# A mixing stage re-ordered in front of a stream of expert weights: modulation sums on TensorE, gate norm on VectorE, attention beside u's projection

## The chip, the cores and the metric

The kernel runs on one core of a Trainium2 chip. The engines of the core are TensorE (PE, matrix products; its weight loads are listed as PEld), VectorE (DVE), ScalarE (ACT), GpSimd (POOL) and SyncE (SP), which in this kernel only issues DMAs, in the order in which they stand in its program. The metric is the time of one execution in microseconds; lower is better. The kernel before takes 1545.3 us (median of three runs, 1542.98 to 1547.39).

## The reference

The reference is one encoder block for 512 tokens of 1024 channels, in float32. Cut to what matters:

```python
mod = silu(c) @ w_ada + b_ada                 # 6 x 1024: shift1, scale1, gate1, shift2, scale2, gate2
h   = rms_norm(x) * (1 + scale1) + shift1
q, k, v, u, g = split(h @ w_in)               # 512, 128, 128, 512, 512 columns
attn = windowed_attention(q, k, v, sink)      # 8 heads, 2 of keys, blocks of 128 tokens and their neighbours
gm   = gelu(u) * (W_s @ layer_norm(gelu(g)) + b_s)      # per chunk of 128 tokens, 8 channel groups
mix  = concat(rms_norm(attn), rms_norm(gm))
x    = x + gate1 * rms_norm(mix @ w_out)
h2   = rms_norm(x) * (1 + scale2) + shift2
aff  = softmax(h2 @ w_router)                 # 16 experts, each takes its 64 best tokens
y    = sum over experts of aff * (silu(xs @ w_gate) * (xs @ w_up)) @ w_down
out  = x + gate2 * rms_norm(y)
```

Each of the 16 experts has three matrices of 1024 x 2816 floats, so the weights of the experts make nearly all of the 593.6 MB that are read from HBM.

## The kernel before

The program has two stages. The first (to about 261 us) holds everything up to the router. The second runs the 16 experts one after the other; for each, the weights come in chunks of 1408 KB (128 partitions x 2816 floats), TensorE multiplies the chosen rows by them, and the chunk's buffer is then free for a later chunk.

**Buffers of the weights.** There are 13 slots in four pools: `sl` (6 slots), `s2p` (3), `s3p` (3) and `s4p` (1). The first stage uses the same bytes: `sl` holds the rows of w_in, w_ada and w_out as they come in; the bytes of `s2p` are taken from the pool of the early phase (`ea`), and its three slots hold `wz`, the rows of w_out for the gMLP's half of the channels, split in two parts, until the last product with them (`project_z`); `s3p` takes over the bytes of the attention's pool `at`, and `s4p` those of `ow`, the output projection's pool. SP issues the chunks in the order of the program and waits at each until the slot's last reader is through (L835). Chunks 0 to 5 go into `sl`, 6 to 8 into `s2p`, 9 to 11 into `s3p`, 12 into `s4p`; 13 and 14 go into three places left over from the first stage (`in_places`, L931 and L932), and from chunk 15 on a slot has to be freed by an expert's product.

**The first stage.** Products that need float32's accuracy are made as three products of split operands (`mm3`, L346 to L348: high by high, low by high, high by low), each with 512 columns. In order of the program:

- `SEQ` orders, for each of the 8 groups k of 128 input channels, `m` (shift1 and scale1 of the group), `d` (the normed and modulated rows hh, hl) and `q` (the products for q, k, v, tile `qkp`). For k in `MODPE` the sums of `m` are products on TensorE (`mod1_rows`, L293, tile `pm`); for k = 4, 6, 7 they are a chain of eight sums on VectorE (`mod1_acc`, L315 and L317, tile `acc1`), which TensorE then only adds over the partitions (`mod1_cols`, L322).
- Eight units of g (tile `pg`, 12 products each), and beside them on VectorE the sums of the other four modulations (`mod2`, L553 and L555, tile `racc`: 8 instructions of 128x1024 for one of the four vectors); `mod2_cols` (L278, L285, L561 to L574) turns the finished sums into columns.
- Eight units of u (tile `pu`), the first four ahead of the attention and the last four in its steps 0 to 3. `gate_norm` is the layer norm of g, for each of four token blocks: BN_STATS and BN_AGGR, an inverse root of one column, a TENSOR_SCALAR (L505) on VectorE, and a product and a sum on GpSimd (L506, L507).
- A loop of 26 steps i. Steps 0 to 15 are `attn_scores`: block n = i // 4, heads j and j + 4 (products `sp` L430; mask and minimum on VectorE, L432; exponential on ScalarE, L435; the division by the sum on GpSimd, L439). Two steps later `attn_out` transposes the probabilities (`ptr`, L454) and multiplies them by v (`po`, L462). A table `todo` hangs the rest of the stage on steps: the rows of w_out (`OWS`), gelu, the spatial products and the change of pools (step 4), `gmlp_cols` and `project_z` (`ZC`), the end of a block's attention and its projection, the residual, the router's logits (`XC`) and, at `RS`, ranks of the first three blocks (`rank_part`, L806).
- `rsqrt` is an inverse root by a guess from the bits and three Newton steps on VectorE, 8 instructions for one column (L184, L186, L191, L196), 11 for more.

So each engine's order is the order in which the program is written; the numbers in the tables decide it, and an engine that waits holds up whatever stands behind.

Of the kernel before, what the change touches and what calls it, by code (L numbers as in the profile page):

```python
# [47 lines left out]
TINY = 2.0 ** -126  # L48


@with_exitstack
def encoder_block(ctx, tc, x, c, w_ada, b_ada, norm_pre_mix, norm_post_mix, w_in, sink, sgu_ln_g,
# [32 lines left out]
    # ---------------------------------------------------------------- loads  # L85
# [17 lines left out]
    # columns of w_ada for shift1, scale1 of 128 channels with the rows of w_in for q, k, v of these channels  # L103
# [18 lines left out]
    def more_loads():  # L122
# [15 lines left out]
        nc.sync.dma_start(lnb, sgu_ln_b.to_broadcast([P, DG]))  # L138
        wst = slot([NG, P], name="wst")
# [4 lines left out]
    # ---------------------------------------------------------------- constants  # L144
# [4 lines left out]
    ones = cp.tile([P, 1], F32, name="ones")  # L149
# [19 lines left out]
    def make_dist():  # L169
        """|distance|, or a huge number outside the window; keys in front of, of, behind the block"""  # L170
# [66 lines left out]
    # ---------------------------------------------------------------- x: transposed; 1 / rms  # L237
# [29 lines left out]
    # ---------------------------------------------------------------- shift1, scale1; h  # L267
# [7 lines left out]
    def mod_rows(pm, col, w, n, first, last):  # L275
        """w [P, 4, n]: four column tiles of the array add col^T w at once"""
# [4 lines left out]
    def mod_cols(rows, n):  # L281
        """the four rows of rows [P, n] as columns: [P, n / 128, 4] in PSUM"""
# [5 lines left out]
    def mod1_rows(k):  # L288
        """PE: even and odd rows of w_ada in column tiles of their own"""
# [17 lines left out]
    acc1 = {}  # L307

    def mod1_acc(k):
        """DVE: the sums over a partition's rows"""  # L310
        acc1[k] = t = ea.tile([P, 2, P], F32, name="acc1", bufs=2)
        for kk in range(KD):
            w = wq[k][0][:, :, kk]
            if kk == 0:
                nc.vector.tensor_scalar(t, w, cs[:, kk:kk + 1], None, op0=OP.mult)  # L315
            else:
                nc.vector.scalar_tensor_tensor(t, w, cs[:, kk:kk + 1], t, op0=OP.mult, op1=OP.add)  # L317

    def mod1_cols(k):
        pm = bank("pm")  # L320
        for j in range(2):
            nc.tensor.matmul(pm[32 * j:32 * j + 32, :P], ones.to_broadcast([P, 32]), acc1[k][:, j], start=True,  # L322
                             stop=True, tile_position=(0, 32 * j))
# [41 lines left out]
    for b in range(NB):  # L365
        sumsq(ssx[:, b:b + 1], x_sb[:, b], junk)
        if b == NB - 1:
            x_rsqrt(b, NB)
# [250 lines left out]
    for k in range(4):  # L619
        unit("u", k)  # L620
        if k < 2:
            mod2_cols(k)
# [462 lines left out]
```

## Time and profile before

| | |
|---|---|
| median of three runs | 1545.3 us (1542.98 to 1547.39) |
| span of the profiled execution | 1544.5 us |
| mean granted TensorE clock | 0.985 |
| TensorE busy | 1387.1 us, 90% |
| VectorE busy | 429.7 us, 28% |
| ScalarE, GpSimd busy | 188.9 us, 116.0 us |
| moved by DMA | 596.86 MB, mean 386 GB/s |

The span runs from the first to the last instruction of the profiled execution, and no time of its own beyond the span is given for it; the median of the timed runs lies 0.8 us above the span. Busy shares are means over two stages that have little in common: in the experts' stage the DMA engines move about 429 GB/s without a break, in the first stage they move between 7 and 355 GB/s. The rows further below are therefore mostly from stretches of the first stage.

### The profile page before, as it was taken

What the parts mean: (1) busy time and instruction counts of PE and PEld (TensorE: products, weight loads), DVE (VectorE), ACT (ScalarE), POOL (GpSimd) and SP (SyncE); (2) the same over time, 40 slices, a digit from 0 to 9 for tenths busy, and PEclk for the clock granted to TensorE, in tenths of its full rate; (3) what the DMA queues carried; (4) which work ended last, traced back from release to release, by engine and by line L of the source; (5) the groups of instructions that cost most, each with busy time, mean ns of one, the idle gap of its engine ahead of it and who ended that gap; (6) DMA issues with size and microseconds to landing.
All of it is one profiled execution on the core that took longest, in us unless ns stands there. A gap on an engine that the chain in (4) does not pass through costs nothing.

```text
span 1544.5 us, 17570 instructions
## 1 busy us (share of the span) xinstructions
PE 1387.1 (90%) x7282; PEld 619.8 (40%) x7282; DVE 429.7 (28%) x1087; ACT 188.9 (12%) x404; POOL 116.0 (8%) x144
## 2 busy tenths in 40 slices
PE   7888998999999998998898998989898989898986
PEld 5665665343444433333333333324242423333323
DVE  5789857112112120212112111112020303020104
ACT  3336433000010000000100000000000000000001
POOL 2457310000000000000000000000000000000002
PEclk9998999999999999999999999999999999999998
DMA  9776608999999999999999999999999999999995
GB/s 316 275 252 181 241 6 334 415 411 428 429 429 429 429 429 428 429 428 429 429 428 429 429 429 429 429 428 429 429 428 429 429 429 429 428 429 429 429 396 202
DMA packets 92711, 596.86 MB, mean 386 GB/s; under 512 B 8692, under 2 KB 31960, under 8 KB 44760
## 3 DMA queue, kind: packets, MB, share of 16 engines
q1 hardware_dynamic: 92632, 595.74, 93.3%
q8 instruction: 57, 0.93, 0.2%
q14 instruction: 22, 0.18, 0.0%
HBM read 593.62 MB, written 2.10 MB: 386 GB/s over the span
## 4 chain that ended last, share of the span: by engine, by line
DMA 60%; PE 28%; DVE 8%; issue 1%; ACT 1%; POOL 1%; SPq 0%; DVEq 0%; ACTq 0%; POOLq 0%
DMA w<-in_w_down_dram 23%; DMA w<-in_w_up_dram 19%; DMA w<-in_w_gate_dram 18%; PE pf L949 11%; PE pd L991 4%; PE px L888 1%; PE pys L1001 1%; PE py L348 1%; PE py L346 1%; PE po L462 1%; PE py L347 1%; DVE ex L851 1%; PE pd L1031 1%; DVE racc L555 1%; DVE acc L317 1%
## 5 line engine op out<-in xcount | busy, mean ns | idle before, releaser
L949 PE MATMUL pf<-w,ex 128*64 128x512 f32 (+1 forms) x3072 | 638.0, 561 | 42.0 <-DMA w<-in_w_up_dram 40.6
L949 PEld LDWEIGHTS pf<-w,ex 128*64 128x64 f32 x3072 | 215.0, 137 | 433.2 <-issue 326.2
L991 PE MATMUL pd<-w,ex 128*64 128x512 f32 (+1 forms) x1440 | 319.3, 563 | 33.7 <-DMA w<-in_w_down_dram 33.7
L991 PEld LDWEIGHTS pd<-w,ex 128*64 128x64 f32 x1440 | 109.9, 136 | 231.7 <-issue 126.0
L967 DVE TENSOR_TENSOR ex<-pf,ex 128x512 f32<-128x512 f32 (+1 forms) x48 | 30.4, 647 | 362.3 <-PE pf L949 362.0
L995 DVE TENSOR_SCALAR ex<-pd,gc 128x512 f32<-128x512 f32 x15 | 11.3, 751 | 377.6 <-PE pd L991 377.6
L907 POOL COPY ex<-ex 128x512 f32<-128x512 f32 x16 | 9.8, 613 | 1138.2 <-DVE ex L905 1058.0
L888 PE MATMUL px<-x_sb,ex 128*64 128x256 f32 x512 | 71.0, 386 | 8.6 <-DVE ex L864 7.4
L919 ACT ACTIVATE ex<-pot 128x512 f32<-128x512 f32 x16 | 9.6, 597 | 544.6 <-PE pot L917 544.6
L1007 DVE TENSOR_TENSOR y<-pys,y 128x512 f32<-128x512 f32 x112 | 68.2, 681 | 17.0 <-PE pys L1001 17.0
L974 ACT ACTIVATE ex<-pht 128x512 f32<-128x512 f32 (+1 forms) x48 | 23.5, 559 | 374.6 <-PE pht L973 374.6
L1001 PE MATMUL pys<-ex 64*128 64x512 f32 x240 | 55.6, 602 | 12.7 <-DVE ex L995 12.7
L900 DVE TENSOR_SCALAR ex<-pxt,mods 128x64 f32<-128x64 f32 x128 | 34.9, 337 | 92.0 <-PE pxt L895 92.0
L888 PEld LDWEIGHTS px<-x_sb,ex 128*64 128x64 f32 x512 | 41.3, 136 | 38.3 <-DVE ex L864 18.8
L851 DVE SCALAR_TENSOR_TENSOR ex<-rt,afs,before 128x512 f32<-128x512 f32 (+2 forms) x65 | 46.8, 719 | 12.3 <-PE rt L858 12.3
L913 DVE COPY gc<-pgc 128x1 f32<-128x1 f32 x16 | 2.5, 158 | 152.6 <-PE pgc L910 152.6
L555 DVE SCALAR_TENSOR_TENSOR racc<-ada,cs,racc 128x1024 f32<-128x1024 f32 x28 | 42.6, 1521 | 0.2
L959 ACT ACTIVATE ex<-pf 128x512 f32<-128x512 f32 (+1 forms) x48 | 26.9, 561 | 121.2 <-PE pf L949 120.4
L1001 PEld LDWEIGHTS pys<-ex 64*128 64x128 f32 x240 | 21.9, 186 | 47.1 <-DVE ex L995 25.9
L973 PE MATMUL pht<-ident,ex 128*128 128x128 f32 x176 | 25.7, 295 | 12.1 <-DVE ex L967 12.1
L973 PEld LDWEIGHTS pht<-ident,ex 128*128 128x128 f32 x176 | 22.7, 213 | 22.7 <-DVE ex L967 22.7
L890 ACT ACTIVATE ex<-px 128x256 f32<-128x256 f32 x32 | 12.3, 383 | 125.7 <-PE px L888 125.6
(254 smaller groups left out, 1086.3 us busy)
## 6 DMA issues: line engine op xcount, KB each, us to landing
w<-in_w_gate_dram SPq DMA_DIRECT2D x128, 1408.0 KB, 26.8
w<-in_w_up_dram SPq DMA_DIRECT2D x126, 1408.0 KB, 26.8
w<-in_w_down_dram SPq DMA_DIRECT2D x120, 1408.0 KB, 26.8
ada<-in_w_ada_dram SPq DMA_DIRECT2D x16, 1024.0 KB, 6.5
w<-in_w_down_dram SPq DMA_DIRECT2D x18, 512.0 KB, 9.6
wq<-in_w_ada_dram SPq DMA_DIRECT2D x16, 512.0 KB, 5.9
wi<-in_w_in_dram SPq DMA_DIRECT2D x4, 1024.0 KB, 5.2
wq<-in_w_in_dram SPq DMA_DIRECT2D x8, 384.0 KB, 6.2
```

Source lines behind the costliest of these rows:

```text
L555: nc.vector.scalar_tensor_tensor(acc[i], t[:, r], cs[:, k:k + 1], acc[i], op0=OP.mult, op1=OP.add)
L851: nc.vector.scalar_tensor_tensor(junk[:, :c1 - c0], p[:, c0:c1], afs[:, b, e:e + 1], before[:, o + c0:o + c1], op0=OP.subtract, op1=OP.is_ ...
L888: nc.tensor.matmul(px[i][h * CAP:(h + 1) * CAP, :256], ohr[:, b], x_sb[:, b, c0:c0 + 256], start=(b == 0), stop=(b == NB - 1))
L900: nc.vector.tensor_scalar(xs[:, k], pt[:, c0:c0 + CAP], s2[:, k:k + 1], sh2[:, k:k + 1], op0=OP.mult, op1=OP.add)
L949: nc.tensor.matmul(pb[n][h * 64:(h + 1) * 64, :NW[n]], XS[e][:, k], t, start=(i == 0), stop=(i == KD - 1))
L959: nc.scalar.activation(hid[:, n * 512:n * 512 + NW[n]], pg[n][:, :NW[n]], AF.Silu)
L967: nc.vector.tensor_tensor(hs, pu[n][:, :NW[n]], hs, op=OP.mult)
L973: nc.tensor.transpose(p[:, j * P:(j + 1) * P], hv[:, j0 + j], ident)
L974: nc.scalar.activation(hT[:, j0:j0 + n], p.rearrange("p (j t) -> p j t", j=4)[:, :n], AF.Copy)
L991: nc.tensor.matmul(pd[dh * 64:(dh + 1) * 64, c0:c0 + n], hT[:, j, h * CAP:(h + 1) * CAP], t[:, o - q * FF:o - q * FF + n], start=(h == 0 a ...
L1001: nc.tensor.matmul(p, OT[e][dh * 64:(dh + 1) * 64, b * P:(b + 1) * P], oe[dh * 64:(dh + 1) * 64, :], start=True, stop=True)
L1007: nc.vector.tensor_tensor(yb, p, yb, op=OP.add)
```

## The change

The changed kernel computes the same. The first stage is put together otherwise:

- `m` is made on TensorE for all eight groups; `mod1_acc`, `mod1_cols` and `MODPE` are gone.
- `mod2(0)` (gate1) is taken up into the q, k, v sequence (`a0` to `a3` in `SEQ`), `mod2(1)` and `mod2(2)` stand beside the units of g, and `mod2(3)` at steps 10 to 13 of the loop (before: 8, 8, 9, 9). The columns of gate1 are made in unit 2 of g, those of shift2 after unit 0 of u, those of scale2 at step 1.
- `gate_norm` takes the four blocks at once, all of it on VectorE, with one inverse root of four columns, after unit 0 of u.
- Two units of u, not four, stand ahead of the attention; the other six stand in steps 0 to 5, and gelu, the spatial products and the change of pools in step 6 (before: 4). `ZC`, `XC`, `OWS`, `GS` and the tables `AE` and `YC` give the other work new steps.
- `attn_out` keeps the transposed probabilities of two steps together, and multiplies them by v in products of 256 columns instead of 128, half as many.
- `rsqrt` takes -v/2 and makes one step of higher order and one Newton step: 6 instructions for one column, 8 for more. The inverse roots of x are taken for four blocks at once.
- The loads of `wst` and of g's first half are issued earlier; the tile `ones` is 160 bytes wide instead of 4, which moves the tiles behind it by 128 bytes. The four pools of weight slots keep their places.

The core of the diff (comments that went, and the same scaling of the argument of `rsqrt` at each of its calls, are left out):

```diff
-MODPE = (0, 1, 2, 3, 5)
-SEQ = "d0 m1 q0 d1 m2 d2 m3 q1 d3 m4 q2 d4 m5 q3 d5 m6 q4 d6 m7 q5 d7 q6 q7"
-M2 = (0, 0, 1, 1, 3)
-M3 = (8, 8, 9, 9, 10)
-GN = (None, None, 0, 0)
-GS, RS = 23, 21
+SEQ = "d0 m1 q0 d1 m2 d2 m3 q1 d3 m4 q2 d4 m5 q3 d5 m6 q4 d6 m7 a0 q5 d7 a1 q6 a2 q7 a3"
+U0 = 2
+GS, RS = 20, 21
+M3 = (10, 11, 12, 13, 15)
+GV = 7
+AE = (5, 11, 13)
+YC = (10, 12, 14, 17)
-ZC = (5, 6, 10, 12)
-XC = (10, 13, 18, 21)
-OWS = (5, 6, 4, 4)
+ZC = (7, 9, 11, 13)
+XC = (13, 15, 18, 21)
+OWS = (8, 9, 6, 7)
...
-    ones = cp.tile([P, 1], F32, name="ones")
+    ones = cp.tile([P, 40], F32, name="ones")[:, 0:1]
...
-            (mod1_rows if k in MODPE else mod1_acc)(k)
+            mod1_rows(k)
...
+            if j % 2 == 0:
+                pTs[g] = at.tile([P, 3, 2, P], F32, name="pT", tag="pT", bufs=2)
...
+        if j % 2:
+            for i in range(nk):
+                for g in range(2):
+                    nc.tensor.matmul(po[n, j][g * HD:(g + 1) * HD, (j - 1) * P:(j + 1) * P],
+                                     v_sb[:, k0 + i, g * HD:(g + 1) * HD], pTs[g][:, i].rearrange("p j q -> p (j q)"),
+                                     start=(i == 0), stop=(i == nk - 1))
...
-        nc.vector.tensor_scalar(v, v, mv[:, 0:1], r, op0=OP.subtract, op1=OP.mult)
-        nc.gpsimd.tensor_tensor(v, v, lng, op=OP.mult)
-        nc.gpsimd.tensor_tensor(v, v, lnb, op=OP.add)
+    def gate_norm():
+        mv = rs.tile([P, NB, 2], F32, name="mv", bufs=1)
+        for b in range(NB):
+            st = rs.tile([P, 6], F32, name="st")
+            nc.vector.bn_stats(st, vn[:, b])
+            nc.vector.bn_aggr(mv[:, b], st)
+            nc.vector.scalar_tensor_tensor(vn[:, b], vn[:, b], mv[:, b, 0:1], lng, op0=OP.subtract, op1=OP.mult)
+        h = rs.tile([P, NB], F32, name="hv", bufs=1)
+        nc.vector.tensor_scalar(h, mv[:, :, 1], EPS, -0.5, op0=OP.add, op1=OP.mult)
+        r = rs.tile([P, NB], F32, name="rln", bufs=1)
+        rsqrt(r, h, NB)
+        for b in range(NB):
+            v = vn[:, b]
+            nc.vector.scalar_tensor_tensor(v, v, r[:, b:b + 1], lnb, op0=OP.mult, op1=OP.add)
...
-        mod2(k // 4, k % 4)
+        mod2(1 + k // 4, k % 4)
+        if k == 2:
+            mod2_cols(0)
...
-    for k in range(4):
+    for k in range(U0):
         unit("u", k)
-        if k < 2:
-            mod2_cols(k)
-        if GN[k] is None:
-            gate_norm(k)
+        if k == 0:
+            mod2_cols(1)
+            gate_norm()
...
-    for k in range(4):
-        at_step(k, (unit, "u", k + 4))
-    at_step(4, (gelu, "u", us[0]), (spatial,), (swap,))
+    for k in range(U0, KD):
+        at_step(k - U0, (unit, "u", k))
+    at_step(1, (mod2_cols, 2))
+    at_step(KD - U0, (gelu, "u", us[0]), (spatial,), (swap,))
```

What stands where is seen in the order of the instructions. On VectorE, where steps 0 and 1 of the attention begin (`st` and `mv`, `vn` and `rln` belong to the gate norm, `racc` to the modulation sums, `pr,am` is the mask of one head pair's scores), the program of before reads:

```order
L432 ISA pr,am<-sp,dist,nsink 128x256
L432 ISA am 128x1
L191 SCALAR_TENSOR_TENSOR rs_t<-rs_y,rs_h 128x1
L555 SCALAR_TENSOR_TENSOR racc<-ada_1190,cs,racc 128x1024
L196 SCALAR_TENSOR_TENSOR rs_y<-rs_t,rs_y 128x1
L437 RECIPROCAL dn<-dn 128x2
L555 SCALAR_TENSOR_TENSOR racc<-ada_1190,cs,racc 128x1024
L191 SCALAR_TENSOR_TENSOR rs_t<-rs_y,rs_h 128x1
L196 SCALAR_TENSOR_TENSOR rs_y<-rs_t,rs_i 128x1
L555 SCALAR_TENSOR_TENSOR racc<-ada_1194,cs,racc 128x1024
L196 SCALAR_TENSOR_TENSOR rln<-rs_t,rs_y 128x1
L191 SCALAR_TENSOR_TENSOR rs_t<-rs_y,rs_h 128x1
```


and the changed program, at the same masks:

```order
L358 TENSOR_SCALAR racc<-ada_899,cs 128x1024
L537 BN_AGGR mv<-st 128x2
L463 ISA pr,am<-sp,dist,nsink 128x256
L463 ISA am 128x1
L360 SCALAR_TENSOR_TENSOR racc<-ada_899,cs,racc 128x1024
L538 SCALAR_TENSOR_TENSOR vn<-vn,mv,sgu 128x512
L360 SCALAR_TENSOR_TENSOR racc<-ada_920,cs,racc 128x1024
L540 TENSOR_SCALAR hv<-mv 128x4
L463 ISA pr,am<-sp,dist,nsink 128x256
L463 ISA am 128x1
L360 SCALAR_TENSOR_TENSOR racc<-ada_920,cs,racc 128x1024
L192 TENSOR_SCALAR rs_i<-hv 128x4
```


In the first, the norm's short instructions for one column stand among the sums of scale2, and the masks of step 0 come behind the statistics of all four blocks; in the second, the masks of step 0 come among the full-width products of the norm, whose one root of four columns follows.

On TensorE, at the last product with `wz`, which frees the last slot of `s2p` (`py` is the output projection, `sp` scores, `ptr` and `po` the attention's output, `pl` logits, `wo` the attention's rows of w_out), the program of before reads:

```order
L347 MATMUL py<-wz,mix 128x512
L348 MATMUL py<-wz,mix 128x512
L346 MATMUL py<-wz,mix 128x512
L347 MATMUL py<-wz_1409,mix 128x512
L348 MATMUL py<-wz,mix 128x512
L430 MATMUL sp<-qk 128x256 x2
L454 MATMUL ptr<-ident,pr 128x128 x4
L736 MATMUL pl_2283<-fold,rows 128x16
L346 MATMUL py<-wo,mix 128x512
L347 MATMUL py<-wo,mix 128x512
L348 MATMUL py<-wo,mix 128x512
```


and the changed one:

```order
L323 MATMUL py<-wz,mix 128x512
L324 MATMUL py<-wz,mix 128x512
L322 MATMUL py<-wz,mix 128x512
L323 MATMUL py<-wz_1462,mix 128x512
L324 MATMUL py<-wz,mix 128x512
L488 MATMUL ptr<-ident,pr 128x128 x4
L714 MATMUL pl<-hT,wsp 32x128 x8
L488 MATMUL ptr<-ident,pr 128x128 x4
L497 MATMUL po<-pT,v_sb 64x256
L722 MATMUL pl_2225<-fold,rows 128x16
L322 MATMUL py<-wo,mix 128x512
L323 MATMUL py<-wo,mix 128x512
```


Before, the scores of the last step (`sp`) stand behind the last product with `wz`; after, they stand ahead of it, and what is left behind it is a shorter rest: 24 products `py` up to the first expert, where it was 36.

## Rows read from the trace of the kernel before

**Rows 1.** Page, part 4: share of the chain that ended last, by engine

```profile
DMA 60%; PE 28%; DVE 8%; issue 1%; ACT 1%; POOL 1%; SPq 0%; DVEq 0%; ACTq 0%; POOLq 0%
```

**Rows 2.** Windows: stretch, length, busy us (x instructions) per engine, PEclk, DMA share, GB/s

```profile
194.00:230.00 36.00, 34.07 (x207) 24.39 (x206) 19.01 (x71) 14.19 (x38) 4.95 (x11) 0.91 0.00 1
230.00:252.00 22.00, 18.34 (x121) 13.32 (x119) 16.38 (x71) 9.75 (x29) 0.93 (x2) 1.00 0.97 383
252.00:254.00 2.00, 1.17 (x6) 1.20 (x7) 1.50 (x3) 1.20 (x3) 0.00 (x0) 0.71 0.27 113
...
400.00:1200.00 800.00, 730.70 (x3704) 284.53 (x3700) 142.83 (x341) 45.16 (x90) 6.13 (x10) 1.00 1.01 429
```

**Rows 3.** Waits of SP's queue, 150 to 275 us: total, times, longest

```profile
SPq L835 <- PE py L348: 49.2, 2, 48.8
SPq L835 <- DVE ty L806: 15.9, 1, 15.9
```

**Rows 4.** Timeline of SP, 225 to 270 us: start, us, line, transfer

```profile
229.85 1.93 SPq L835 DMA_DIRECT2D w<-in_w_gate_dram  x2
231.96 25.53 SPq L835 DMA_DIRECT2D w<-in_w_up_dram  x5
257.54 0.94 SPq L931 DMA_DIRECT2D w<-in_w_up_dram  x1
```

**Rows 5.** Windows of the first stage, columns as in rows 2

```profile
0.00:70.00 70.00, 55.88 (x370) 42.07 (x370) 43.19 (x108) 25.74 (x45) 23.50 (x44) 0.93 0.87 283
70.00:93.50 23.50, 23.32 (x102) 18.54 (x102) 15.91 (x12) 7.19 (x12) 15.15 (x10) 1.00 0.97 355
93.50:131.00 37.50, 32.72 (x152) 22.53 (x150) 37.30 (x77) 13.56 (x26) 22.79 (x16) 0.91 0.63 193
131.00:160.00 29.00, 23.42 (x182) 15.07 (x182) 26.66 (x67) 20.09 (x44) 18.33 (x22) 0.88 0.63 212
160.00:194.60 34.60, 34.09 (x203) 23.45 (x202) 28.80 (x87) 14.31 (x36) 9.91 (x14) 1.00 0.57 210
194.60:231.90 37.30, 35.37 (x211) 25.28 (x210) 19.45 (x73) 14.91 (x40) 4.95 (x11) 0.91 0.04 7
231.90:261.60 29.70, 22.41 (x159) 16.81 (x158) 22.76 (x101) 12.55 (x36) 0.93 (x2) 0.94 0.81 325
```

**Rows 6.** Waits of TensorE, 0 to 70 us: total, times, longest

```profile
PE pm L322 <- DVE acc L317: 4.5, 2, 2.6
```

**Rows 7.** Groups by line, 0 to 262 us: busy, mean ns, idle before

```profile
L555 DVE SCALAR_TENSOR_TENSOR racc<-ada,cs,racc 128x1024 f32<-128x1024 f32 x28 | 42.6, 1521 | 0.2
...
L317 DVE SCALAR_TENSOR_TENSOR acc<-wq,cs,acc 128x256 f32<-128x256 f32 x21 | 13.9, 663 | 0.5
...
L191 DVE SCALAR_TENSOR_TENSOR rs_t<-rs_y,rs_h 128x1 f32<-128x1 f32 x34 | 9.6, 282 | 0.5
...
L506 POOL TENSOR_TENSOR vn<-vn,sgu 128x512 f32<-128x512 f32 x4 | 7.1, 1778 | 4.9 <-DVE vn L505 3.8 <-DVE rs_y L196 0.7 <-DMA ada<-in_w_ada_dram 0.4
...
L293 PE MATMUL pm<-wq,cs 128*32 128x128 f32 x160 | 6.7, 289 | 0.8 <-DMA wq<-in_w_ada_dram 0.8
...
L505 DVE TENSOR_SCALAR vn<-vn,mv,rln 128x512 f32<-128x512 f32 x4 | 3.1, 778 | 0.0
```

**Rows 8.** Timeline of VectorE, 105 to 117 us: start, us, line, operation

```profile
105.74 1.27 DVE L555 SCALAR_TENSOR_TENSOR racc<-ada,cs,racc 128x1024 f32<-128x1024 f32 x1
...
109.56 1.21 DVE L191 SCALAR_TENSOR_TENSOR rs_t<-rs_y,rs_h 128x1 f32<-128x1 f32 x1
...
116.60 0.53 DVE L505 TENSOR_SCALAR vn<-vn,mv,rln 128x512 f32<-128x512 f32 x1
```

**Rows 9.** Timeline of TensorE at 200.6 us, columns as in rows 8

```profile
200.60 0.40 PE L346 MATMUL py<-wz,mix 128*128 128x512 f32 x1
200.84 0.40 PE L347 MATMUL py<-wz,mix 128*128 128x512 f32 x1
```

**Rows 10.** Window of 222 to 229.5 us, columns as in rows 2

```profile
222.00:229.50 7.50, 7.50 (x27) 6.23 (x24) 2.36 (x14) 0.40 (x2) 0.00 (x0) 0.54 0.00 0
```

More of the change, by code (lines that the diff above doesn't have):

```diff
@@ L305, in mod1_end @@
         nc.vector.tensor_tensor(sh1[:, k:k + 1], shift, pcol("ba", k), op=OP.add)
[L307 to L323, printed above, removed]
-        rows = rs.tile([P, P], F32, name="rows", bufs=1)[:64]
-        nc.vector.tensor_copy(rows, pm[:64, :P])
-        pt = bank("pt")
-        nc.tensor.transpose(pt[:, :64], rows, ident[:64, :64])
-        mod1_end(k, pt[:, 0:1], pt[:, 32:33])
     def modulate(k):
@@ L363, in qkv, with mod2 @@
             mm3(qkp[m], h[:, c0:c0 + P], l[:, c0:c0 + P], hh[k], hl[k], k == 0, k == KD - 1)
+    G0 = cp.tile([P, D], F32, name="G0")
+    mods = cp.tile([P, 4, 8], F32, name="mods")
+    g1c, sh2, s2, g2c = (mods[:, i] for i in range(4))
+    rb = cp.tile([P, NE], F32, name="rb")
+    acc = {}
+    def mod2(i, kk):
+        t = slot([2, D], name="ada2")
+        nc.sync.dma_start(t, ada[:, 2 * kk:2 * kk + 2, 2 + i])
+        if kk == 0:
+            acc[i] = (ea if i < 2 else at).tile([P, D], F32, name="racc")
+        for r in range(2):
+            k = 2 * kk + r
+            if k == 0:
+                nc.vector.tensor_scalar(acc[i], t[:, r], cs[:, k:k + 1], None, op0=OP.mult)
+            else:
+                nc.vector.scalar_tensor_tensor(acc[i], t[:, r], cs[:, k:k + 1], acc[i], op0=OP.mult, op1=OP.add)
@@ new lines, in mod2_cols @@
+    def mod2_cols(i):
+        pm = bank("pm2")
+        mod_rows(pm, ones, acc[i].rearrange("p (j w) -> p j w", j=4), 256, True, True)
+        rows = at.tile([P, 256], F32, name="rows2", tag="pT", bufs=2)
+        nc.vector.tensor_copy(rows, pm[:, :256])
+        m = mod_cols(rows, 256)
+        nc.vector.tensor_tensor(mods[:, i].rearrange("p (j q) -> p q j", j=4), m,
+                                pcol("ba", 16 + 8 * i, 8).rearrange("p (j q) -> p q j", j=4), op=OP.add)
+        if i == 0:
+            nc.vector.tensor_tensor(g1c, g1c, pcol("pom", 0, 8), op=OP.mult)
+            spread(G0, g1c)
+        elif i == 2:
+            nc.vector.tensor_tensor(s2, s2, pcol("npf", 0, 8), op=OP.mult)
+            pb = bank("pb")
+            for k in range(KD):
+                mod_rows(pb, sh2[:, k:k + 1], wr[:, k:k + 1].to_broadcast([P, 4, NE]), NE, k == 0, k == KD - 1)
+            nc.vector.tensor_scalar(rb, pb[:, :NE], -1.0, None, op0=OP.mult)
+            nc.vector.scalar_tensor_tensor(wsp[:, :, :NE], wr, -1.0, s2.unsqueeze(2).to_broadcast([P, KD, NE]),
+                                           op0=OP.mult, op1=OP.mult)
+        elif i == 3:
+            nc.vector.tensor_tensor(g2c, g2c, pcol("pof", 0, 8), op=OP.mult)
@@ L365, in encoder_block, with spread @@
+    def spread(dst, cols):
+        for i in range(2):
+            p = bank("spr")
+            for k in range(4):
+                kk = i * 4 + k
+                nc.tensor.matmul(p[:, k * P:(k + 1) * P], cols[:, kk:kk + 1].to_broadcast([P, P]), ident,
+                                 start=True, stop=True)
+            nc.scalar.activation(dst[:, i * 512:(i + 1) * 512], p, AF.Copy)
     for b in range(NB):
@@ L766, in encoder_block @@
         at_step(M3[k], (mod2, 3, k))
[L767 removed]
     at_step(M3[4], (mod2_cols, 3))
[L769 to L772 removed]
     for n in range(NB):
[L774 to L777 removed]
+        for i, f in enumerate(((gmlp_cols, n), (project_z, n, 0), (project_z, n, 1))):
+            at_step(ZC[n] + i, f)
@@ L793, in gate2 @@
+        for i, f in enumerate(((x2_cols, n), (logits, n), (affinity, n))):
+            at_step(XC[n] + i, f)
     def gate2():
```

174 lines of the change are left out of this document (51 added, 123 removed).

## The prediction

> **What bounds the kernel now.** I read the chain of waits first. It belongs to DMA with 60% [rows 1]: the program ends when the last expert weights have come. The windows of the experts' stage show 429 GB/s with the DMA engines full [rows 2], so nothing is gained there; the time is the moment from which the stream runs without a break, plus a rest that stays the same. That moment is found by going backwards along SP. At 230 us SP has waited 48.8 us on a product `py` (L348), the last reader of the `wz` slots [rows 3]; from 194 to 230 us DMA moved 1 GB/s [rows 2]. The waiting chunk goes at 229.85, the next at 231.96, and six chunks (6 to 11) flow. Chunk 12 then waits on VectorE (L806, 15.9 us in all [rows 3]) and goes at 257.54 [rows 4]. The six chunks are through by about 252.5: 22 us at 97% and 383 GB/s, then 27% in the next two microseconds [rows 2]. So 5 us more are empty. From 257.5 on the stream is whole, and 1544.5 - 257.5 = 1287 us are the fixed rest. Two numbers decide: when the last `wz` product ends (W, 231.9 now), and how long after W chunk 12 can go (25.6 us now).
>
> The windows of the first stage tell what sets W [rows 5]. In q, k, v (0 to 70) and g (70 to 93.5) TensorE does 55.9 and 23.3 us. From 93.5 to 131 VectorE is busy 37.3 of 37.5 us and from 131 to 160 26.7 of 29, while TensorE's clock is granted at 0.91 and 0.88 only: VectorE bounds that part. From 194.6 to 231.9 TensorE is busy 35.4 of 37.3 us and bounds it.
>
> **Step 1, q, k, v.** TensorE's two waits for the sums of `acc` go, -4.5 us [rows 6], and the slower clock behind them (0.93 in the mean [rows 5]), an estimate of -1.5. Three groups more are summed on TensorE: 32 products each, 160 of them take 6.7 us [rows 7], so 3 x 1.34 = +4.0, less about 0.8 for the two products and the transposition of the old form. VectorE loses the 21 sums L317, 13.9 us [rows 7], and gets the eight sums of gate1 back, 8 x 1.27 = 10.2 [rows 8], ahead of the end of the stretch, where it is busy 43 of 70 us. Sum -2.8 (bounds -6 and +1): the end of q, k, v at 67.2.
>
> **Step 2, g.** This stretch is TensorE's (23.32 of 23.5). Gate1's columns and their spreading come in from the u part: some 14 small products, about 0.29 each by L293's mean, +3.5 with one wait for a copy (bounds +2, +5). The four loads of gate1 now stand on SP ahead of g's second half: 4 MB, 12 us at the 355 GB/s of this stretch, while DMA is busy 0.87 of the 70 us before and has 9 us left; I take nothing for it (bounds 0, +3). g ends at 67.2 + 23.5 + 3.5 = 94.2, so the first two steps cancel, and what follows starts where it did, 93.5 give or take 3.
>
> **Step 3, VectorE from the first statistics of the norm to the masks of step 11** (93.5 to 194.6 before: busy 37.30 + 26.66 + 28.80 = 92.8 of 101.1 us). In the order the same stretch afterwards has:
> - 17 sums `racc` instead of 24: -7 x 1.27 = -8.9 [rows 8]; at the mean of 1.52 [rows 7] -10.6.
> - one root of four columns instead of four of one: 8 short instructions for 36, by 0.15 each -4 (L191 shows 0.28 [rows 7], which would be -8).
> - two full products a block on VectorE where there was one: 4 more, 0.53 alone [rows 8] to 0.78 [rows 7], +2.6. The GpSimd pair leaves altogether.
> - work that now stands behind step 11 (two residuals, two part sums of the projection, three roots): ten of 128x512 and some 38 short ones, 6.5 + 6.1 = -12.6. This is moved, not saved.
>
> Together -23: 69.9 us. At the same fill (101.1 / 92.8) that is 76 us: step 11 at 169.6, where it was at 194.6. TensorE has 48 products `py` between steps 2 and 11 where it had 84, and u's last units stand ahead of step 6, so it waits more; I add nothing for its clock, since the stretch whose fill I use already had 0.88 to 0.91. Taken: 170 (163 to 177).
>
> **Step 4, TensorE from step 11 to W.** Before, 72 products `py` and the rest of three steps in 37.3 us. Afterwards 120 `py`, and the scores of step 15, four sums of squares, eight transpositions and gate2's columns. One `py` takes 0.233 us start to start [rows 9], so +11.2, and +4.5 for the others by their means, less 0.5 for the joined `po`: +15.2, of 27.5 us of such row times before. Of the 37.3 us before, 7.5 ran at a clock of 0.54 [rows 10], which costs about 3.4; a denser stretch may be spared that. 37.3 + 15.2 = 52.5: W at 170 + 52.5 = 222.5 (bounds 215 without the slow clock and with an early step 11, 230 with both against it).
>
> **Step 5, from W to the stream.** The six chunks need 20.6 us from W (252.5 - 231.9). Chunk 12 needs the last reader of the output projection's pool, 25.6 us from W before; behind W stand now 24 `py` instead of 36 and no scores, -12 x 0.233 - 1.6 = -4.4 of TensorE's 22.4 in 29.7 us [rows 5], with its waits -5: 20.6. Both come at the same time, so chunk 12 goes at W + 20.6 to 22, and the empty 5 us go.
>
> **Sum.** Chunk 12 at 222.5 + 20.6 = 243.1, before 257.5: -14.4. The end has one root of four columns, three short instructions fewer, -0.5. The span is 1544.5 - 14.9 = 1529.6; the median lies 0.8 above the span, so 1530.4: **1530 us**. What loads are moved costs nothing by this sum: chunks 0 to 5 wait for the sums of gate2, now at steps 10 to 13 (about 165 to 185); they need 20 us, and W is after 215. If they came later than W they would push the six behind them, at 3.4 us a chunk.
>
> [...] L506 on GpSimd took 1.78 us [rows 7], a sum of one column on VectorE 1.21 beside it [rows 8], where L191 has 0.28 in the mean, and `racc` 1.52 in the mean [rows 7] against 1.27 alone [rows 8]: the two engines hold each other up. [...]
>
> **Rivals.**
> - *The products of the norm collide with GpSimd.* Each of the eight takes up to L506's 1.78 instead of 0.65, 0.6 more on average, +5 on the engine that bounds step 3: 1535. For it: rows 8. Against it: GpSimd is freed of 14 us there. 0.12.
> - *Only the 5 us of step 5 come.* Masks, exponential, division and transposition of a step wait for each other in order; what is taken from VectorE turns into waiting, and step 11 comes at 179: W 231.9, 1544.5 - 5.0 - 0.5 = 1539, with the 0.8 1540. For it: from 160 to 194.6 VectorE was busy only 28.8 of 34.6. 0.13.
> - *Slower: TensorE falls to its lower clock in steps 2 to 11.* With less `py` there it has some 32 us of work (48 x 0.233 and ten steps of scores, transpositions and `po`) in the 45 us that step 3 leaves these steps. [...] For it: every thin stretch above lost clock. Against it: the thinnest, 131 to 160, still had 0.88. 0.08.
> - *More:* the fill of steps 0 to 11 rises because the short roots no longer stand between the masks; step 11 at 163, W at 213: 1520. 0.12.
> - The wider `ones` moves tiles by 128 bytes but no slot of the stream; a change of the 429 GB/s would be worth 3 us per GB/s over 1287 us, and I see no cause for one.
>
> **How the numbers follow.** Forecast 0.55 (its own range 1523 to 1537), collision 0.12, only the gap 0.13, slower clock 0.08, more 0.12. The range from 1517 to 1543 leaves out the slower case and the far end of the better one. What a measurement can tell from no change is 0.3%, 4.6 us, so faster means under 1540.7. Of "only the gap" some 0.06 fall to no change; of the slower case 0.02. Faster 0.84, same 0.08, slower 0.08.
>
> **What would show it.** Right: the profile after has no wait of TensorE on `acc`; the masks of step 11 at 163 to 177; W at 215 to 230, with TensorE over 90% busy from step 11 to W; no empty DMA between chunk 11 and 12; 429 GB/s as before. Wrong: a granted clock under 0.7 between steps 2 and 11, VectorE products of the norm well over 0.8 us, or SP's first expert chunks issued after 190 us.

## The result and the profile after

The changed kernel takes 1525.1 us (median of four runs, 1522.92 to 1526.64) against 1544.85 us for the kernel before beside it: a ratio of 0.986, 95% interval 0.9837 to 0.9882, 19.75 us faster. The profiled execution spans 1524.1 us, 20.4 less than before. Forecast were 1530 and a gain of 14.9 in the span.

The stream starts earlier. SyncE's timeline of the changed kernel (start, us, line, transfer; it answers to [rows 4]):

```profile
212.58 1.03 SPq L815 DMA_DIRECT2D w<-in_w_gate_dram  x2
214.68 20.54 SPq L815 DMA_DIRECT2D w<-in_w_up_dram  x5
235.27 0.84 SPq L911 DMA_DIRECT2D w<-in_w_up_dram  x1
...
249.00 0.33 SPq L815 DMA_DIRECT2D w<-in_w_up_dram  x1
```

The row of L911 is chunk 13; chunk 12 is the last of the five in the row above it. The last `wz` product ends at W = 214.6 (231.9 before), and chunk 13 goes at 235.3, which is 20.7 us behind W (25.6 before). These two are -17.3 and -4.9; the remaining time from chunk 13 to the end became 1.8 longer (1288.8 against 1287.0). SP still waits for VectorE ahead of chunk 12 (first row; [rows 3] has 15.9), but the wait ends about when the six chunks ahead are through, and DMA is empty for some 1.4 of the 4 us of the second row, where the kernel before has 4.6 of the 5 us of the third:

```profile
SPq L815 <- DVE ty L786: 13.9, 1, 13.9
```

```profile
234.00:238.00 4.00, 0.71 (x7) 0.48 (x3) 3.07 (x18) 0.40 (x2) 0.00 (x0) 0.95 0.64 215
```

```profile
252.50:257.50 5.00, 3.59 (x27) 2.60 (x27) 4.11 (x17) 1.93 (x5) 0.00 (x0) 0.66 0.08 30
```

The windows of the changed kernel by stage (columns as in [rows 2]; the first five rows answer to the first six of [rows 5]):

```profile
0.00:64.50 64.50, 55.06 (x454) 41.60 (x454) 28.36 (x77) 25.81 (x46) 24.10 (x45) 0.97 0.96 320
64.50:91.40 26.90, 26.27 (x129) 20.59 (x129) 21.97 (x20) 8.10 (x13) 14.26 (x9) 1.00 0.98 358
91.40:124.00 32.60, 29.18 (x193) 20.95 (x191) 30.58 (x53) 13.08 (x24) 14.40 (x10) 0.95 0.71 199
124.00:165.00 41.00, 37.89 (x202) 24.32 (x202) 38.29 (x93) 25.39 (x65) 25.10 (x32) 1.00 0.55 198
165.00:214.60 49.60, 46.23 (x268) 33.86 (x267) 34.45 (x118) 22.77 (x61) 8.05 (x14) 1.00 0.23 84
...
235.00:240.00 5.00, 1.45 (x7) 0.93 (x8) 3.81 (x24) 0.40 (x2) 0.00 (x0) 0.76 0.81 299
239.40:242.00 2.60, 2.58 (x12) 1.64 (x14) 2.33 (x12) 0.00 (x0) 0.06 (x1) 0.50 0.98 412
242.00:246.40 4.40, 4.29 (x28) 2.61 (x24) 0.45 (x2) 1.19 (x3) 0.55 (x1) 0.73 1.01 417
246.40:249.00 2.60, 2.60 (x15) 1.04 (x16) 1.65 (x7) 0.86 (x1) 0.00 (x0) 1.00 0.15 61
400.00:1200.00 800.00, 731.28 (x3716) 284.48 (x3712) 146.21 (x353) 45.79 (x91) 6.16 (x10) 1.00 1.01 429
```

The reader is to see four things. The first stretch is full of DMA now (0.96 of the time, 0.87 before). From 91.4 to 165, u and the attention to step 11, TensorE and VectorE are both over 89% busy at a clock of 0.95 to 1.00; before, the clock stood at 0.88 to 0.91 in most of it. The experts' stage moves the same 429 GB/s. And the end of the stage has a longer wait, in the three rows ahead of the last: when the first expert's rows are chosen (`px`), TensorE is granted half its clock (0.50, then 0.73), so the first expert's product (`pf`) starts late, chunk 15 waits for it until 249.0, and DMA, through with chunk 14, falls to 61 GB/s. The wait itself is not new. In the kernel before chunk 15 goes at 269.16, 11.6 us behind chunk 13, where it is 13.7 now, and DMA falls short there too:

```profile
254.00:256.00 2.00, 2.00 (x19) 1.40 (x21) 1.61 (x8) 0.73 (x3) 0.00 (x0) 0.50 0.01 6
...
261.60:266.50 4.90, 4.76 (x36) 2.92 (x36) 2.75 (x14) 1.14 (x3) 0.61 (x1) 1.00 1.00 415
...
269.00:271.00 2.00, 2.00 (x14) 0.68 (x12) 0.00 (x0) 0.00 (x0) 0.00 (x0) 1.00 0.60 148
```

There the clock had fallen ahead of `px` (0.50 from 254 to 256) and was back at 1.00 when `px` began, so that `px` to `pf` took 4.9 us; in the changed kernel it takes 7.0.

### The profile page after: what moved, and what is told of

The parts are those of the page before. It is cut to its first block, busy times and chain, and to the rows that moved or that the text cites. A ratio compares the mean times of both kernels' runs of the same rounds, so it can differ in the third digit from the quotient of the medians.

```text
span 1524.1 us, 17489 instructions
## 1 busy us (share of the span) xinstructions
PE 1374.7 (90%) x7286; PEld 610.7 (40%) x7286; DVE 407.0 (27%) x1001; ACT 185.7 (12%) x402; POOL 106.4 (7%) x136
## 4 chain that ended last, share of the span: by engine, by line
DMA 63%; PE 29%; DVE 5%; ACT 1%; issue 1%; SPq 0%; DVEq 0%; ACTq 0%
DMA w<-in_w_down_dram 23%; DMA w<-in_w_up_dram 20%; DMA w<-in_w_gate_dram 20%; PE pf L929 10%; PE pd L971 4%; PE px L868 1%; PE py L324 1%; PE py L322 1%; PE py L323 1%; PE pys L981 1%; DVE ex L831 1%; PE pd L1011 1%; PE qkp L322 1%; PE qkp L323 1%; PE qkp L324 1%
## 5 line engine op out<-in xcount | busy, mean ns | idle before, releaser
L929 PEld LDWEIGHTS pf<-w,ex 128*64 128x64 f32 x3072 | 215.0, 137 | 433.2 <-issue 326.1
L954 ACT ACTIVATE ex<-pht 128x512 f32<-128x512 f32 (+1 forms) x48 | 23.5, 559 | 374.3 <-PE pht L953 374.3
L470 POOL TENSOR_SCALAR pr<-pr,dn 128x256 f32<-128x256 f32 (+1 forms) x32 | 26.6, 844 | 38.3 <-DVE dn L468 20.7
## 6 DMA issues: line engine op xcount, KB each, us to landing
w<-in_w_gate_dram SPq DMA_DIRECT2D x128, 1408.0 KB, 26.8
w<-in_w_up_dram SPq DMA_DIRECT2D x126, 1408.0 KB, 26.7
w<-in_w_down_dram SPq DMA_DIRECT2D x120, 1408.0 KB, 26.7
```

What stands on the lines that cost most here:

```text
L929: nc.tensor.matmul(pb[n][h * 64:(h + 1) * 64, :NW[n]], XS[e][:, k], t, start=(i == 0), stop=(i == KD - 1))
```

## The experiments

Every kernel was timed beside the kernel before; the ratio and its interval are from those runs. From each profile the table gives the starts of the last q, k, v product and of the last `wz` product, their difference, and the rest from there to the end of the span. The difference is the better measure, since the start of the program alone scatters by 3 us: the q, k, v of the kernel before and of e12, alike in program, start their last one at 69.6 and 72.8.

| kernel | median us | ratio, 95% | q,k,v end | last wz | difference | rest |
|---|---|---|---|---|---|---|
| before | 1544.85 | 1 | 69.6 | 231.5 | 161.9 | 1313.0 |
| changed | 1525.1 | 0.986, 0.9837-0.9882 | 64.1 | 214.3 | 150.1 | 1309.8 |
| e5, changed again | 1522.9 | 0.9838, 0.9819-0.9858 | 61.9 | 211.0 | 149.1 | 1308.2 |
| e1 sums on VectorE | 1533.7 | 0.9906, 0.9885-0.9927 | 68.0 | 220.9 | 152.9 | 1310.7 |
| e2 norm on GpSimd | 1528.7 | 0.988, 0.986-0.990 | 62.5 | 216.7 | 154.2 | 1310.0 |
| e3 four units of u first | 1523.3 | 0.9842, 0.9823-0.9862 | 62.4 | 210.5 | 148.1 | 1309.7 |
| e4 fillers | 1521.9 | 0.9834, 0.9814-0.9853 | 62.1 | 212.2 | 150.1 | 1306.9 |
| e6 e3 + e4 | 1520.4 | 0.9823, 0.9805-0.9842 | 64.0 | 212.1 | 148.2 | 1308.6 |
| e7 po apart | 1530.3 | 0.9884, 0.9864-0.9903 | 62.4 | 218.5 | 156.1 | 1311.1 |
| e8 ones 4 bytes | 1538.8 | 0.994, 0.9923-0.9957 | 64.8 | 215.0 | 150.2 | 1322.2 |
| e9 s3p aligned | 1525.7 | 0.9856, 0.9839-0.9873 | 62.1 | 212.3 | 150.2 | 1310.1 |
| e10 e6 + e9 | 1520.7 | 0.9825, 0.981-0.9841 | 62.4 | 210.5 | 148.1 | 1307.8 |
| e11 before, sums on TensorE | 1543.9 | 0.9972, 0.9959-0.9984 | 63.8 | 226.9 | 163.1 | 1315.2 |
| e12 before, po joined | 1549.2 | 1.0007, 0.9996-1.0017 | 72.8 | 234.2 | 161.4 | 1314.8 |

**e1, the sums of q, k, v's modulation back on VectorE.**

```diff
+MODPE = (0, 1, 2, 3, 5)
...
-            mod1_rows(k)
+            (mod1_rows if k in MODPE else mod1_acc)(k)
...
+            if k not in MODPE:
+                mod1_cols(k)
```

> The changed kernel with one part undone: shift1 and scale1 of groups 4, 6 and 7 are again summed by eight instructions each on VectorE. Theory (each stage hands on to the next, so what is late in q, k, v is late at the end): q, k, v end near 69 instead of 64.5 us, the last product with wz at 218 to 220 instead of 214.6, the time 4 to 6 us above the changed kernel's 1525. Rival (the part of the first stage that VectorE bounds has its own start, the sums of the other modulations, and takes the 4 us up): the last product with wz at 215 to 216, the time within 1.5 us. Second rival: VectorE has 15 us more ahead of gate1's sums, so it is later than q, k, v's own delay: 8 us or more.

The last `wz` product came at 220.9, against 211.0 to 214.3 of the changed kernel: 7 to 10 later, 4 to 6 of it in q, k, v. The ratio rose by 0.005 to 0.007, 7 to 11 us. TensorE's waits on the sums are back, the same as in [rows 6]:

```profile
PE pm L322 <- DVE acc L317: 4.5, 2, 2.6
```

The rival that takes the delay up falls. The first theory holds for q, k, v, but the delay at W and in the time is larger than its own 4 to 6 us: 3 to 4 us more arise behind q, k, v, in the direction of the second rival.

**e11, the same part alone, in the kernel before:** `MODPE` holds all eight groups.

> The kernel before with one part of the change alone: shift1 and scale1 of all eight groups summed on TensorE. Theory (undoing this part in the changed kernel cost 7 to 8 us in the last product with wz, 5.5 of it in q, k, v): q, k, v end 4 to 6 us earlier, and since VectorE has nothing to wait for but g's end, the last product with wz 4 to 6 us earlier, time -4 to -6. Rival (VectorE bounds what follows and has no less to do there): last product with wz within 1.5 us, time the same.

4.3 us faster, 2.5 to 6.3 by the ratio's interval; the last `wz` product 4.6 earlier. The first theory again. The part brings 4 to 5 us by itself, and some 8 where the rest of the change follows it.

**e2, the norm's product and sum back on GpSimd.**

```diff
-            nc.vector.scalar_tensor_tensor(vn[:, b], vn[:, b], mv[:, b, 0:1], lng, op0=OP.subtract, op1=OP.mult)
...
-            nc.vector.scalar_tensor_tensor(v, v, r[:, b:b + 1], lnb, op0=OP.mult, op1=OP.add)
+            nc.vector.tensor_scalar(v, v, mv[:, b, 0:1], r[:, b:b + 1], op0=OP.subtract, op1=OP.mult)
+            nc.gpsimd.tensor_tensor(v, v, lng, op=OP.mult)
+            nc.gpsimd.tensor_tensor(v, v, lnb, op=OP.add)
```

> The changed kernel with the norm's root still taken for four blocks at once, but the product with the norm's weight and the sum with its bias again on GpSimd (eight instructions of 128x512), and one TENSOR_SCALAR a block on VectorE. Theory (VectorE bounds the attention's steps, and the eight full products cost it 8.1 us in the changed kernel's trace, four TENSOR_SCALARs 2.5 to 3): if VectorE gained the difference cleanly the time would fall by 3 to 5 us; since the GpSimd instructions hold it up by 0.5 us or more each, it stays within 2 us. Rival (leaving GpSimd is a main source of the gain): the splits of u's weights and the division of the probabilities queue behind 14 us of GpSimd work, masks of step 11 come 5 us later or more, time +5 or more.

3 to 6 us slower, the difference 4 to 5 longer, the masks of step 11 at 169.7, against 162.4 (e5) and 165.7 of the changed kernel: the rival is right, near the lower end of its size. (The ratio's interval lies above that of e5 and overlaps that of the first measurement.) The window from u's first product to its last in e2, and TensorE's longest wait there:

```profile
89.70:130.20 40.50, 32.38 (x205) 22.26 (x203) 34.09 (x61) 15.41 (x33) 28.76 (x24) 0.87 0.64 190
```

```profile
PE pm L277 <- DVE racc L360: 7.7, 1, 7.7
```

and the same window in the changed kernel (e5):

```profile
89.20:118.80 29.60, 26.19 (x123) 18.61 (x121) 29.46 (x49) 11.74 (x22) 14.39 (x10) 1.00 0.65 188
```

The first is longer than the delay, since u's last unit stands behind the scores of step 3 in e2; up to the scores of step 2, e2 takes 34.6 us and e5 31.0. In these shorter stretches the sums for shift2 and scale2 on VectorE read (instructions, busy us, mean ns; e2, then e5):

```profile
L360 DVE SCALAR_TENSOR_TENSOR racc<-ada,cs,racc 128x1024 f32<-128x1024 f32 x10 | 17.8, 1776 | 0.0
```

```profile
L360 DVE SCALAR_TENSOR_TENSOR racc<-ada,cs,racc 128x1024 f32<-128x1024 f32 x10 | 13.6, 1356 | 0.0
```

With GpSimd busy 26.2 us up to the scores of step 2 instead of 14.4, the same ten sums take VectorE 4.2 us longer, TensorE waits 7.7 us for them (2.7 at the longest in e5), and its clock falls to 0.87. In the changed kernel the collision shows too: the four products that stand among u's splits take 1346 ns, the four later ones 748. Of the four, the one beside no GpSimd instruction took 0.73 us, and one beside a split 1.78:

```profile
L538 DVE SCALAR_TENSOR_TENSOR vn<-vn,mv,sgu 128x512 f32<-128x512 f32 x4 | 5.4, 1346 | 0.0
...
L545 DVE SCALAR_TENSOR_TENSOR vn<-vn,rln,sgu 128x512 f32<-128x512 f32 x4 | 2.7, 748 | 0.0
```

```profile
101.34 0.73 DVE L538 SCALAR_TENSOR_TENSOR vn<-vn,mv,sgu 128x512 f32<-128x512 f32 x1
...
104.33 1.78 DVE L538 SCALAR_TENSOR_TENSOR vn<-vn,mv,sgu 128x512 f32<-128x512 f32 x1
```

```profile
103.51 2.05 POOL L319 TENSOR_TENSOR wl<-wi,wh 128x512 fp32r<-128x512 f32 x1 [3.71 <-ACT wh L318]
```

**e3, four units of u ahead of the attention:** `U0 = 4`.

> The changed kernel with four units of u ahead of the attention, as before, instead of two; gelu, spatial products and the change of pools are then at step 4. In TensorE's order 15 products more stand ahead of the first scores and 20 fewer between the scores of steps 1 and 2. Theory (VectorE is full in this part with sums and norm, so an earlier first mask is worth little; the scores of step 2 come behind u's last products in both): masks of step 0 about 4 us later, those of step 11 within 2 us of 165.7, time within 2 us. Rival (attention beside u is the source of the gain): masks of step 11 at 170 or later, time +4 to +8.

The difference is 1 to 2 us shorter than in the changed kernel, the time within its runs. So that attention begins two units of u sooner is no source of the gain.

**e7, the products of the probabilities apart.** `attn_out` as in the kernel before, but for the split of the last block's heads.

> The changed kernel with the probabilities of a step multiplied by v by themselves again: 160 products of 128 columns instead of 80 of 256. Theory (TensorE bounds the part behind the masks of step 11, and 80 products less are worth what they took: 160 took 17.8 us of recorded time in the kernel before, 80 take 13.0 in the changed one, some 22 of the 80 pairs behind step 11): last product with wz 1 to 2 us later, time +1 to +2. Rival (joining two steps delays the first one's output by a step, and ScalarE's copies are what the products wait for, 4.7 us in the changed kernel): earlier output, time -1 to -3.

7.4 us slower than e5 on the same chip, the difference 7.0 longer; the direction of the theory at four to seven times its size; the rival falls. Steps 2 to 11 and step 11 to W, of e7 and then of e5:

```profile
120.80:166.00 45.20, 42.67 (x315) 27.48 (x314) 39.65 (x98) 26.68 (x65) 25.39 (x32) 1.00 0.56 204
166.00:218.90 52.90, 50.56 (x296) 37.26 (x295) 33.88 (x117) 22.81 (x61) 5.95 (x13) 0.97 0.18 71
```

```profile
118.90:162.00 43.10, 39.72 (x272) 25.57 (x272) 39.51 (x98) 26.94 (x66) 25.27 (x32) 1.00 0.59 212
162.00:211.40 49.40, 46.03 (x268) 33.86 (x265) 34.23 (x118) 22.53 (x61) 7.79 (x14) 1.00 0.22 82
```

VectorE's work is the same; TensorE has 7.5 us more, and is 94% to 96% busy. A part of it is the order of the instructions, e7 and then e5 on TensorE:

```profile
142.11 0.91 PE L461 MATMUL sp<-qk 64*128 64x384 f32 x2
142.95 0.43 PE L493 MATMUL po<-pT,v_sb 128*64 128x128 f32 x2
143.31 0.91 PE L461 MATMUL sp<-qk 64*128 64x384 f32 x2
144.15 0.87 PE L485 MATMUL ptr<-ident,pr 128*128 128x128 f32 x6
```

```profile
138.78 0.92 PE L461 MATMUL sp<-qk 64*128 64x384 f32 x4
139.63 0.55 PE L488 MATMUL ptr<-ident,pr 128*128 128x128 f32 x3
```

Four score products of 64 rows each, two for each head, take 0.85 us when they stand together; two of them take 0.84 when `po` stands between (from a row's start to the start of what follows). In e7's order this happens in four steps, in the changed kernel's in one: 2.5 us by these figures.

**e12, the same part alone, in the kernel before** (with gate2's columns at step 11 and the last block split 2 and 2).

> The kernel before with one part of the change alone: the probabilities of two steps joined for the products with v (the last block's projection then splits 2 and 2 heads instead of 3 and 1, and gate2's columns are made a step later). Theory (undoing it in the changed kernel cost 7 us because TensorE bounds there from the first steps on; in the kernel before VectorE does up to step 11): last product with wz 1 to 3 us earlier, time -1 to -3. Rival (the products are dear wherever they stand): -6 to -8, as in the changed kernel.

No gain: 1.0007. The difference is 0.5 shorter. Neither the theory's 1 to 3 us nor the rival's 6 to 8 came. Three windows of e12, which answer to the fourth to sixth of [rows 5], 3.2 us later because q, k, v ended so much later:

```profile
134.20:163.20 29.00, 22.22 (x150) 12.44 (x149) 22.78 (x57) 18.92 (x40) 16.58 (x21) 0.75 0.64 204
163.20:198.00 34.80, 33.35 (x165) 23.09 (x166) 30.23 (x83) 16.35 (x42) 10.40 (x14) 0.97 0.58 216
198.00:234.60 36.60, 35.41 (x215) 24.63 (x213) 21.71 (x85) 14.72 (x40) 4.98 (x11) 1.00 0.03 7
```

VectorE's work is the same in sum (74.7 us, before 74.9). From the end of q, k, v the masks of step 11 come 3.0 us later than in the kernel before, and from there W comes 3.5 us sooner. In the first part, where TensorE has less to do and waits, its clock was granted at 0.75 and 0.97, against 0.88 and 1.00; in the second at 1.00, against 0.91. The two score halves are split in three of the steps by its order, in two before. That the joined products pay only where TensorE bounds fits this; how much of the loss and of the gain is due to the clock, the order or the products is not shown.

**e8, `ones` 4 bytes wide, and e9, all slots aligned.** In e8 the tile is `cp.tile([P, 1], ...)` again.

> The changed kernel with the tile ones 4 bytes wide again, which moves the tiles behind it back by 128 bytes. Theory (the slots of the weight stream don't move, so nothing changes): 429 GB/s between 400 and 1200 us, time within 1 us. Rival (aligned buffers are a part of the gain): slower streams or slower engines on the moved tiles, time +2 or more.

The theory falls, and it fell with its premise, for the slots do move: 15.9 us slower than e5, the first stage as in the changed kernel (difference 150.2), the rest 12 to 14 us longer. (In the profiles, the first stage of e8 also starts 2.9 us later than that of e5.) The small tiles lie in front of the slots of `sl`, `s2p` and `s4p`; the new root needs 128 bytes less of them, so that with the narrow `ones` these ten slots begin at 128 of 256 bytes, and with the wide one at 0, as in the kernel before. The stream of e8:

```profile
400.00:1200.00 800.00, 726.01 (x3670) 280.21 (x3667) 142.18 (x340) 45.20 (x90) 6.15 (x10) 1.00 1.01 425
```

The prediction's 3 us per GB/s make 12 us of these 4 GB/s.

e9 keeps `ones` narrow, but makes up for it elsewhere, and moves the three slots of `s3p`, which lie at 224 of 256 bytes in both kernels:

```diff
+    rp = ctx.enter_context(tc.tile_pool(name="rp", bufs=1, side="right"))
+    nc.gpsimd.memset(rp.tile([P, 56], F32, name="pad"), 0.0)
...
-        lg = rs.tile([P, NE], F32, name="lg")
+        lg = rs.tile([P, NE], F32, name="lg", bufs=1)
```

(and likewise `mx` and `sm`.)

> The changed kernel with all 13 slots of the weight stream starting at a multiple of 256 bytes. Before and after, the ten slots of sl, s2p and s4p do so and the three of s3p start 32 bytes below one; here a pad of 224 bytes at the other end moves s3p, and ones is 4 bytes wide, so that the small tiles in front of the slots lie where they lay in the run that was 16 us slower. Theory (that run lost 4.2 of 428.8 GB/s because its ten slots began 128 bytes off): 16 us for ten slots are 1.6 us a slot, so three more slots aligned give about 5 us, near 430.2 GB/s between 400 and 1200 us, time 1517 to 1519, a ratio to before of 0.981. Rival (the 16 us came from the small tiles that moved): as slow as that run, 424 to 425 GB/s, +16. Second rival (only an offset of 128 costs, not one of 224): no change.

```profile
400.00:1200.00 800.00, 731.46 (x3720) 285.11 (x3719) 146.81 (x354) 45.84 (x91) 6.49 (x11) 1.00 1.01 429
```

429 GB/s and the changed kernel's time: the second rival. The narrow `ones` and the tiles behind it cost nothing (e9), the slots' start does: with ten of 13 slots 128 bytes off, e8 streams at 425 GB/s for 429, 0.9% less, while the three slots 32 bytes below a boundary, aligned in e9, gained nothing there. From issue to landing a chunk of 1408 KB takes 26.7 to 26.8 us in the median in the changed kernel and in e9, and 27.0 us in e8. Why 128 bytes cost and 224 do not stays open.

**e4, fillers at the router.** `fill(n)` makes n products of 128x512 into a bank that nobody reads: two after `spread(G1, g2c)`, one each around the last block's `pl2`, one ahead of `px`.

> The changed kernel with five products of 128x512 whose result nobody reads, put where TensorE waits at the router: two behind the spreading of gate2, one each around the last block's logits, one ahead of the first expert's row selection. Theory (in the changed kernel the clock was granted at 0.50 from 239.4 to 242 us, px took 6.1 us against 4.1, chunk 15 waited for the first expert's product until 249.0 and DMA ran dry from 246.4 to 250): with TensorE kept busy the clock stays, px to pf takes 5 us instead of 7, and the time falls by 1.5 to 2.5 us. Rival (the fillers themselves hold up the chain to px, a little under 1 us each): px later by 1 to 3 us, time the same or +2.

The windows of e4 from `px` to chunk 15:

```profile
237.20:239.40 2.20, 2.13 (x19) 1.51 (x20) 2.13 (x12) 0.00 (x0) 0.00 (x0) 1.00 0.96 394
239.40:242.20 2.80, 2.69 (x21) 1.49 (x20) 0.73 (x3) 1.20 (x3) 0.61 (x1) 1.00 1.02 424
242.20:244.80 2.60, 2.60 (x15) 1.03 (x16) 1.64 (x7) 0.85 (x1) 0.00 (x0) 1.00 0.96 397
```

The clock stays at 1.00, and `px` to the first expert's product takes 4.9 us. It takes 4.9 in all three kernels with fillers, and 6.3 to 7.4 in the eight kernels of the changed form without them. `px` itself comes no later behind the last `wz` product (25.1 us, 25.2 in the changed kernel and in e5), so the rival falls; the step and the clock are as the theory says. What it is worth is less sure: the rest is 1306.9, 1308.6 and 1307.8 in the kernels with fillers, 1309.4 in the mean of the changed kernel, e5, e3 and e9, which is 1.7 us less; but e5 alone has 1308.2, and the times of e4 (1521.2 to 1522.8) lie within those of e5 (1521.3 to 1525.4) but for 0.1 us.

**e6 and e10, what gained put together:** e6 is e3 with e4, e10 is these two with e9.

> The changed kernel with both of the edits that gained by themselves: four units of u ahead of the attention, and five products that nobody reads in TensorE's waits at the router. Theory (the two act at different places, one ahead of the last product with wz and one behind it): the gains add, 5 to 7 us under the changed kernel, a ratio to before near 0.982. Rival (each time the same 2 us were won, DMA decides behind): no better than either alone, 0.983 to 0.984.

> The aligned slots together with four units of u ahead of the attention and the five products that nobody reads at the router. Theory (three places, three sums): 5 us for the slots and 2 to 3 for the other two, time 1514 to 1517, ratio 0.979. Rival (a faster stream makes the first stage's end no earlier, and the edits at the router were worth nothing by themselves): as the aligned slots alone.

e6 runs 1519.57 to 1522.57, e5 beside it 1521.3 to 1525.38; e10 1520.07 to 1521.46, e9 beside it 1523.76 to 1526.93. So e6 and e10 are 2.4 and 5.0 us under a kernel of the changed one's form; the intervals of the ratios overlap for e6 and just about for e10. Neither sum came out as expected: e6 is short of the 5 to 7 us, and e10 does not reach 1514 to 1517. They have the lowest medians here, and the aligned `s3p` adds nothing.

## Why the prediction was right, and where its sizes were off

- **The frame was right.** The stream's start decided: chunk 13 goes 20.7 us behind W (forecast 20.6 to 22, under the name of chunk 12: the row at 257.54 that the prediction reads as chunk 12 is chunk 13, and 12 goes 0.4 us ahead of it). SP's wait for the sums of ranks has not gone (13.9 us, 15.9 before); it now ends when the six chunks are through, and some 1.4 us of DMA are empty where it was 4.6. The engines did what was expected of the likeliest case: scores of step 11 at 164.7 and their masks at 165.7 (forecast 170, 163 to 177), W at 214.6, just outside the 215 to 230 that were named, TensorE 93% busy between them. No stretch before W has a clock under 0.95, so the slower clock that has 0.08 of the chances did not come. The measured 1525.1 lies on the better side of the forecast's own range, towards the rival that expected more. Steps 1, 3 and 4 were each too long by nearly 3 us and the end too short by 2; these are the 5.5 us between 1529.6 and 1524.1. (The W of 213 in that rival is not the sum of its terms: 163 and 52.5 are 215.5.)
- **Step 1 was mis-sized**: -2.8 forecast, -5.4 in the profile (69.9 to 64.5) of which the scatter of the start is a part, 4.3 by e11, and some 8 at W by e1. It charged the three groups more with TensorE time in full, +4.0. TensorE's busy time did not grow (55.9 us before, 55.1 now) though it makes 84 products more: its clock rose from 0.93 to 0.97, and the products fill its waits. DMA is at 0.96 of the stretch now and may be what limits it; no run shows that. That g takes the 3.5 us more was right (23.5 to 26.9).
- **Steps 3 and 4 were too long by 3 us each** (73.3 us for 76, 49.9 for 52.5). In step 3 VectorE's work was right to 1 us (68.9 for 69.9); what differs is the fill, 94% where the 92% of before were kept. The term that was too small is the joined `po`, put at -0.5 and in step 4 alone: e7 shows -7 over the two. It was counted as TensorE work beside a bounding VectorE; with VectorE relieved TensorE, too, is 92% busy from step 2 on. e12 shows that the same edit is worth nothing in sum where it is not so. In step 4 the clock is a second cause: the 3.4 us that the low clock of [rows 10] had cost were kept in the 37.3, and the clock now stays at 1.00.
- **The collision came, but its price was wrong.** One of the named signs of being wrong did come, products of the norm well over 0.8 us: four of the eight take 1346 ns among GpSimd's splits, and all eight 8.1 us where 0.65 each had been put, 2.9 more instead of the rival's 5. But the alternative is dearer, 3 to 6 us by e2.
- **The sum of the end was wrong**, -0.5 forecast, +1.8 measured: the rest was taken as fixed, though it holds the first expert's start. `px` begins 4.1 us behind chunk 13 in both kernels, but takes 2.1 us longer to `pf` now, at the clock of 0.50 and 0.73. e4 shows the clock in it.
- **`ones` was judged rightly, but not understood.** The slots lie where they lay and stream alike, as the prediction says; that the wide tile is what keeps them there was not seen, and e8, whose theory denied it, shows that without it the change would have lost 13 to 16 of its 20 us.
- One sentence ahead of the prediction is wrong: the order on an engine is not the program's. The build orders instructions itself, u's last units stand ahead of step 2's scores in the trace, behind them in the program, and an edit like e7 moves the scores too.

Undone one at a time, the parts are worth about 8 (e1), 4 to 5 (e2) and 7 (e7) at W, together some 19 for the 17.3 found. This is no exact division, since a part's worth depends on the others (e7 and e12). The new place of u's units is worth none (e3). The shorter roots, the new place of gate1's sums and the new steps of the projection were not tried by themselves.

## What to carry to other kernels

Where two engines bound by turns, a saving on one can be worth nothing alone (e12, ratio 1.0007) and several us once the other is relieved (e7, 7 us): size a part after the other parts. What lies behind the last wait is not fixed; ask what is late next when that wait ends sooner, and what clock it will find (0.50 at `px` here). When small tiles are added or removed, look where the buffers of the main stream begin (e8, 12 to 14 us in the rest).

## What was not expected of the hardware

- Ten of 13 slots beginning 128 bytes off a multiple of 256 cost 0.9% of a stream at 429 GB/s, some 13 us (e8); aligning the three slots 32 bytes below one brought nothing that can be measured (e9).
- Two heads' score products (64*128 in the trace, two for each head) took 0.85 us for both heads where they stand together (e5), and 0.84 us for each two of the four where products of `po` stand between (e7).
- TensorE was busy 1.45 us between 235 and 240 us of the changed kernel, and its granted clock was 0.76 in the mean there and 0.50 from 239.4 to 242; with five products that nobody reads it was granted at 1.00 from 230 to 244.8 (e4).
- The same sum of 128x1024 on VectorE took 1.36 us in the mean in a stretch of 31.0 us with GpSimd busy for 14.4, and 1.78 in one of 34.6 us with GpSimd busy for 26.2 (e5 and e2, ten sums each).
